# S5 over pairs of tokens, with its complex products on VectorE and other durations for the planner

## The chip, the cores and the metric

The kernel runs on one core of one Trainium2 chip. The time is the device time of one execution in microseconds (us); the median of several runs counts, and a difference of 0.2% (3.2 us) is about the least that can be told from none. A profile is taken of one further execution. Its columns of time start at the start of that execution's span.

## The reference

One layer of a hybrid streaming encoder for 256 tokens of 2048 channels, in fp32: an RMS norm, a wide input projection (w_in), three token mixers side by side (S5, HGRN2, mLSTM), a branch product for each mixer merged under sigmoid gates, an output projection, and a feed-forward part with a short causal convolution. The mixer that changes is S5, a diagonal complex state space: 32 groups of 16 channels, 64 states a group.

```
dt = exp(log_dt);  a = exp((lam_re + i lam_im) * dt)          # per group and state
c  = (a - 1) / lam;  bb = c * b                                # complex
x_t = bb @ u_t                                                 # 16 channels -> 64 states
s_t = a * s_{t-1} + x_t                                        # 256 tokens
y   = Re(c_out @ s) + d * u;  y = gelu(y);  y = y * sigmoid(y @ w_glu + b_glu)
```

## The kernel before

**Main work.** Every product with a large weight runs in three fp32r matmuls: SP loads a block of the weight (raw), ScalarE rounds it to a high half (wh, `act` at L115), VectorE subtracts to get the low half (wl, `tt` at L123), and TensorE adds high x high, high x low and low x high into a PSUM bank (mp). Blocks of 8 x 128 rows ("subs") follow one another; the halves of a block are made two blocks ahead (SPLIT), and loads run three jobs ahead (LOAD). Each engine works through its own queue in the order in which the program was written, so an early side instruction with a late input holds up what stands behind it.

**Side work.** The mixers are Python generators (`s5`, `hgrn`, `ml_...`). Between main matmuls, `pump` takes the next step of the first generator that can go on, as long as the planner's clock of VectorE or ScalarE is not more than LEAD = 2.25 us ahead of TensorE's. This clock (`Clock`, and the costs in `act`, `cost`, `scan`, `mm`, `transpose`) exists only while the program is written; it decides the order of the instructions and nothing else. `until(eng, t)` makes a generator wait till the planned clock of an engine reaches t. `drain(name)` empties a generator before a job that needs its result: the S5 results (yah, yal) are needed by the first `branch_job` of branch "a", the HGRN2 results by branch "b".

**S5.** The scan over complex states is made real by turning: with a = mag e^{i th}, the states are turned back by th t, scanned with the real mag, and turned forward. GpSimd computes the parameters (`s5_parameters`, with pw, the cosines and sines of th, 2 th, 4 th and so on), the scaled output matrix Cw, and three of four tables of cos(th t), sin(th t) for 256 tokens (`table`, one for each quarter q of the states, 4 blocks of 128); VectorE makes the first table. For each quarter, `stack` lays out u three times (high, low, high) in fp32r beside the input matrix s5b, so that TensorE gets an fp32-like product in one fp32r matmul (`emit_bu`, 4 for each half quarter). Each of eight half quarters ("units") then takes, on VectorE, four products of 128x512 from PSUM (m1, m2), two sums, four scans of 256 tokens and two products of 128x1024, and on GpSimd two sums; `c_products` multiplies with Cw (output of 32 rows for each block, four blocks side by side in TensorE), `skip` adds d u. GELU, the gate (w_glu, fp32) and the split into yah and yal end S5; the HGRN2 generator goes on after it.

**Beside S5** run the first 42 jobs: u, HGRN2's f and q, V, mLSTM's cx and v, and the first eight gates. Their results leave PSUM in late steps on VectorE (times R1) and ScalarE.

Of the kernel before, what the change touches and what calls it, by code (L numbers as in the profile page):

```python
# [17 lines left out]
LN_EXP = "natural_log_exp_and_others"  # L18

P = 128  # L20
# [28 lines left out]
class Clock:  # L49


    def __init__(self):
        self.t = {"pe": 0.0, "act": 0.0, "dve": 0.0, "pool": 0.0}

# [13 lines left out]
def hybrid_trunk(ctx: ExitStack, tc: tile.TileContext, a, dbg=None, stop=None):  # L68
# [5 lines left out]
    POWERS_AT = 25.0  # L74
# [63 lines left out]
    def scan(out, d0, d1, init, op0, op1, after=0.0):  # L138
        nc.vector.tensor_tensor_scan(out=out, data0=d0, data1=d1, initial=init, op0=op0, op1=op1)  # L139
        return ck.run("dve", after, 0.08 + 0.0021 * width(out))  # L140

    def mm(out, lhsT, rhs, start, stop, after=0.0):
        nc.tensor.matmul(out, lhsT, rhs, start=start, stop=stop)  # L143
        per = 0.000425 if lhsT.dtype == F32R else 0.0017
        return ck.run("pe", after, 0.002 + per * width(rhs))

    def transpose(out, in_, ident, after=0.0):
        nc.tensor.transpose(out, in_, ident)  # L148
        return ck.run("pe", after, 0.22)
# [51 lines left out]
    def split(job, c0, n):  # L201
        raw = job["raw"]
        wh = sb([P, RAW // 2], F32R, "wh", bufs=3)
        wl = sb([P, RAW // 2], F32R, "wl", bufs=3)
        t = act(wh[:, :n], raw[:, c0:c0 + n], AF.Copy)
        tt(wl[:, :n], raw[:, c0:c0 + n], f32(wh[:, :n]), SUB, after=t)
        return wh, wl

    gens = []

# [20 lines left out]
    def drain(name, key=None):  # L231
# [3 lines left out]

        while open_yet():
            before = dict(ck.t)
            pump(upto=name)
            if before == ck.t and open_yet():
# [3 lines left out]
                else:  # L243
                    raise RuntimeError(f"{name} waits for what never comes")

    def until(eng, t):
        while ck.t[eng] < t:
            yield "wait"
# [6 lines left out]
    LOAD, SPLIT, LEAD = 3, 2, 2.25  # L255

    def run_jobs():
# [32 lines left out]
        for i, (j, k) in enumerate(subs):  # L290
# [12 lines left out]
            wh, wl = parts[i]  # L303
            parts[i] = None
            work = job["subs"][k][2](wh, wl)
# [92 lines left out]

    def total(out, ps):
# [7 lines left out]
    def project():  # L407
# [3 lines left out]
        def evac_u(m):  # L411
            def f(ps):
# [3 lines left out]
                ready[f"u{m}"] = tt(v["u"][:, m, :], ps, R1, MULT, after=ck.t["pe"] - 2.6)  # L416
# [93 lines left out]
    def s5_parameters():  # L510
# [83 lines left out]
        ar, ai, cr, ci = t16("ar"), t16("ai"), t16("cr"), t16("ci")  # L594
        gt(ar, mag, pw[:, 0, 0, :], MULT)
        gs(ar, ar, -1.0, ADD)
        gt(ai, mag, pw[:, 1, 0, :], MULT)
        gt(cr, ar, lre, MULT)
# [8 lines left out]
        Cr0 = page(14, [P, 2, 16, 32], name="s5craw")  # L607
        nc.sync.dma_start(out=Cr0, in_=a["s5c"])
        ncr, nci = t16("ncr"), t16("nci")
        gs(ncr, cr, -1.0, MULT)  # L610
        gs(nci, ci, -1.0, MULT)
        Cr0 = page(14, [P, 2, 16, 32], name="s5craw")
        nc.sync.dma_start(out=Cr0, in_=a["s5c"])

        Cw = page(13, [P, 2, 16, 32], name="s5c")
        tq = page(11, [P, 16, 32], name="s5cq")
        for o, x0, x1 in ((0, cr, nci), (1, nci, ncr)):
            gt(Cw[:, o], Cr0[:, 0], bc(x0.unsqueeze(2), [P, 16, 32]), MULT)
            gt(tq, Cr0[:, 1], bc(x1.unsqueeze(2), [P, 16, 32]), MULT)
            gt(Cw[:, o], Cw[:, o], tq, ADD)  # L620
        v["s5"] = (mag, pw, Cw, POWERS_AT)

    def s5():
        mag, pw, Cw, tp = v["s5"]
        tabs = {}

        def table(q, tm, eng="pool"):
            tb = half(q % 2, "s5tab").rearrange("p (r b) t -> p r b t", r=2)
            e = nc.vector if eng == "dve" else nc.gpsimd
            e.memset(tb[:, 0, :, 0:1], 1.0)  # L630
            e.memset(tb[:, 1, :, 0:1], 0.0)
            for j in range(8):
                n = 1 << j
                c, s = (bc(pw[:, x, j, 4 * q:4 * q + 4].unsqueeze(2), [P, 4, n]) for x in (0, 1))
                for x, y, op in ((0, 1, SUB), (1, 0, ADD)):
                    new = tb[:, x, :, n:2 * n]
                    tt(tm[:, :, :n], tb[:, y, :, 0:n], s, MULT, eng=eng, after=tp)
                    tt(new, tb[:, x, :, 0:n], c, MULT, eng=eng)
                    t = tt(new, new, tm[:, :, :n], op, eng=eng)
                if eng == "dve":  # L640
                    yield
            tabs[q] = (tb, t)

        yield from until("dve", tp)
        yield from table(0, page(9, [P, 4, P], name="s5tm"), "dve")
        BT = page(14, [P, 1536], name="s5bt")
        braw, tm = BT[:96, :1024], BT[:, 1024:].rearrange("p (b t) -> p b t", b=4)
        for _ in table(1, tm):
            pass
        yg = v["u"]  # L650
        units = [(q, h) for q in range(4) for h in range(2)]
        bu, wg = {}, []

        stacked = {}

        def stack(q):

            nc.sync.dma_start(out=braw, in_=a["s5b"][:, q])
            us = page((3, 6)[q % 2], [96, 4, T], F32R, name="s5us")
            bs = page(12, [96, 2, 4, P], F32R, name="s5bs")  # L660
            uh, ul = scratch(dt=F32R, name="s5uh"), scratch(name="s5ul")
            t = act(uh, v["u"][:, q, :], AF.Copy)
            yield from until("dve", t)
            t = tt(ul, v["u"][:, q, :], f32(uh), SUB)
            for x in (0, 2, 1):
                for b in range(4):
                    part = ul if x == 1 else v["u"][:, q, :]
                    t = act(us[32 * x:32 * x + 32, b, :], part[32 * b:32 * b + 32, :], AF.Copy, after=t if x == 1 else 0.0)
                    yield
            bsf = bs.rearrange("p r b n -> p (r b n)")  # L670
# [3 lines left out]
            stacked[q] = (us, bs, max(t, t2))  # L674
            yield

        def emit_bu(i):
            q, h = units[i]
            if h == 0:
                yield from wait_for(f"u{q}")  # L680
                yield from stack(q)
            us, bs, t = stacked[q]
            yield from until("pe", t)
            banks = yield from side(2)
            out = [b.rearrange("p (r t) -> p r t", r=2) for b in banks]
            for b in range(2):
                for r in range(2):
                    mm(out[b][:, r, :], bs[:, r, 2 * h + b, :], us[:, 2 * h + b, :], True, True)
            bu[i] = (banks, out)

        def c_products(q, ss, tdone):
            yield from until("pe", tdone)
            bank = yield from side()
            yps = bank[:, :T]
            for r in range(2):
                for b in range(4):
                    mm(yps[32 * b:32 * b + 32, :], Cw[:, r, 4 * q + b, :], ss[b // 2][:, r, b % 2, :], r == 0, r == 1)
            v["ypre"] = (bank, yps, q, ck.t["pe"])
# [7 lines left out]
        yield from emit_bu(0)  # L706
        pend, ss = None, []
        for i, (q, h) in enumerate(units):
            tb, ttab = tabs[q]
            yield from until("dve", ttab)  # L710
            if pend is not None:
                yield from c_products(*pend)
                pend = None
            m1 = page(8 + i % 2, [P, 2, 2, T], name="s5m1")
            for b in range(2):
                cb = bc(tb[:, 0, 2 * h + b, :].unsqueeze(1), [P, 2, T])
                tt(m1[:, :, b, :], bu[i][1][b], cb, MULT, after=ck.t["pe"])
                yield
            m2 = page(10 + i % 2, [P, 2, 2, T], name="s5m2")
            for b in range(2):  # L720
                sbb = bc(tb[:, 1, 2 * h + b, :].unsqueeze(1), [P, 2, T])
                tt(m2[:, :, b, :], bu[i][1][b], sbb, MULT)
                yield
            shut(*bu.pop(i)[0])
            if i == 5:
# [3 lines left out]
            if i + 1 < len(units):  # L729
                yield from emit_bu(i + 1)  # L730
            else:
                for j, pg in enumerate((12, 10)):
# [6 lines left out]
            for r in range(2):  # L739
                for b in range(2):  # L740
                    blk = 4 * q + 2 * h + b
                    scan(m2[:, r, b, :], bc(mag[:, blk:blk + 1], [P, T]), m1[:, r, b, :], 0.0, MULT, ADD)
                    yield
            cb = bc(tb[:, 0, 2 * h:2 * h + 2, :].unsqueeze(1), [P, 2, 2, T])
            sbb = bc(tb[:, 1, 2 * h:2 * h + 2, :].unsqueeze(1), [P, 2, 2, T])
            tt(m1, m2, cb, MULT)
            yield
            t = tt(m2, m2, sbb, MULT)
            tt(m1[:, 0], m1[:, 0], m2[:, 1], SUB, eng="pool", after=t)
            t = tt(m1[:, 1], m1[:, 1], m2[:, 0], ADD, eng="pool")  # L750
            ss.append(m1)
            if h == 1:
                pend, ss = (q, ss, t), []
                if q + 2 < 4:
                    for _ in table(q + 2, tm):
                        pass
# [8 lines left out]
        for m in range(4):  # L765
# [5 lines left out]
            tp = ck.t["pe"]  # L771
            yield from until("act", tp)
            sg = scratch(name="sg")
# [3 lines left out]
            t = tt(sg, sg, yg[:, m, :], MULT)  # L777
            t = act(v["yah"][:, m, :], sg, AF.Copy, after=t)
            yield
            tt(v["yal"][:, m, :], sg, f32(v["yah"][:, m, :]), SUB, after=t)  # L780
# [542 lines left out]
    def first_norm(load_to, split_to):  # L1323
# [53 lines left out]
        ck.t = {"pe": 9.7, "act": 20.0, "dve": 21.0, "pool": 31.0}  # L1377
# [164 lines left out]
```

## Time and profile before

| | us |
|---|---|
| runs, median of 3 | 1590.81 (1589.32 to 1590.94) |
| the profiled execution | 1589.37 |
| its span | 1587.6 |
| TensorE busy | 1544.3 (97%) |
| VectorE busy | 1122.9 (71%) |
| ScalarE busy | 863.9 (54%) |
| GpSimd busy | 235.0 (15%) |

In the profile PE is TensorE, DVE is VectorE, ACT is ScalarE, POOL is GpSimd and SP the engine that issues most loads. PEclk is the clock that TensorE was granted as a share of 2.4 GHz. An fp32 matmul appears as two records, an fp32r matmul or a transpose as one. In names, s5m are S5's products and states, s5tab its tables, xp the PSUM banks of side work. An idle stretch of an engine is put down to what ended it.

### The profile page before, as it was taken

How to read it: one execution, taken by the hardware profiler on the slowest of the kernel's cores; microseconds unless marked ns; L12 is line 12 of the kernel's file. 1: busy time of each engine (PE TensorE's matmuls, PEld its weight loads, DVE VectorE, ACT ScalarE, POOL GpSimd, SP SyncE). 2: the span in 40 equal slices, each digit the busy share in tenths (PEclk: the TensorE clock that was granted, in tenths of full speed). 3: DMA queues.
4: the chain of work that ended last, by engine and by line, in shares of the span. 5: the costliest groups of instructions: out<-in, count | busy, mean ns of one | idle time of the engine just before them, and what ended most of it. 6: DMA issues, size and time to landing. Idle time of an engine off the chain costs nothing.

```text
span 1587.6 us, 25383 instructions
## 1 busy us (share of the span) xinstructions
PE 1544.3 (97%) x10094; PEld 1406.4 (89%) x10094; DVE 1122.9 (71%) x1638; ACT 863.9 (54%) x1260; POOL 235.0 (15%) x343
## 2 busy tenths in 40 slices
PE   8989889999999999999999999999999999999996
PEld 8989889899899999899888888888888888888886
DVE  7899989687653667576667777777777776454454
ACT  5555355666645557455556555555555565444442
POOL 7967862000000000000110000000000000010110
PEclk9999999999999999999999999999999999999998
DMA  7445445444455444556555555555555555555552
GB/s 266 175 166 176 138 166 186 148 150 142 155 186 212 143 143 160 179 192 241 187 187 184 187 191 191 191 191 188 187 186 186 186 187 188 176 199 177 198 183 100
DMA packets 42375, 284.71 MB, mean 179 GB/s; under 512 B 4865, under 2 KB 5249, under 8 KB 12305
## 3 DMA queue, kind: packets, MB, share of 16 engines
q1 hardware_dynamic: 40336, 276.25, 50.3%
q0 software_dynamic: 1056, 5.34, 1.0%
q8 instruction: 79, 1.29, 0.3%
q10 hardware_dynamic: 864, 1.50, 0.3%
q14 instruction: 40, 0.32, 0.1%
HBM read 280.98 MB, written 2.10 MB: 178 GB/s over the span
## 4 chain that ended last, share of the span: by engine, by line
PE 91%; DVE 5%; ACT 2%; DMA 1%; issue 1%; DVEq 0%; SPq 0%; ACTq 0%
PE mp L143 86%; PE xp L143 5%; DVE wl L123 2%; DMA raw<-w_in 1%; DVE s5m L123 1%; DVE s5m L139 1%; ACT wh L115 1%; DVE cv L135 0%; ACT L115 0%; DVE s5bs L123 0%; PE xp L148 0%; DVE x L123 0%; ACT s5bs L115 0%; ACT s5us L115 0%; DVEq L1537 0%
## 5 line engine op out<-in xcount | busy, mean ns | idle before, releaser
L123 DVE TENSOR_TENSOR wl<-raw,wh 128x1024 fp32r<-128x1024 f32 (+2 forms) x532 | 644.2, 1212 | 402.9 <-ACT wh L115 398.8
L115 ACT ACTIVATE wh<-raw 128x1024 fp32r<-128x1024 f32 (+2 forms) x532 | 549.7, 1034 | 640.8 <-PE mp L143 547.3
L143 PE MATMUL mp<-HX,wh 128*128 128x512 f32 (+1 forms) x3072 | 882.3, 354 | 1.8 <-ACT wh L115 1.2
L143 PE MATMUL mp<-HX,wl 128*128 128x256 f32 x2496 | 687.2, 283 | 15.1 <-DVE wl L123 15.1
L143 PEld LDWEIGHTS mp<-HX,wh 128*128 128x128 f32 x3072 | 535.7, 190 | 76.2 <-ACT wh L115 1.8
L143 PEld LDWEIGHTS mp<-HX,wl 128*128 128x128 f32 x2496 | 472.0, 189 | 27.9 <-DVE wl L123 17.7
L143 PE MATMUL mp<-g,wh 128*128 128x512 f32 (+1 forms) x748 | 246.3, 382 | 0.0
L143 PE MATMUL mp<-g,wl 128*128 128x256 f32 x704 | 195.4, 281 | 0.0
L143 PEld LDWEIGHTS mp<-g,wh 128*128 128x128 f32 x748 | 136.7, 188 | 28.1
L143 PE MATMUL mp<-wh,HX 128*128 128x256 f32 (+1 forms) x768 | 141.1, 284 | 0.0
L143 PEld LDWEIGHTS mp<-g,wl 128*128 128x128 f32 x704 | 132.5, 188 | 1.3
L143 PEld LDWEIGHTS mp<-wh,HX 128*128 128x128 f32 x768 | 120.3, 190 | 0.8 <-issue 0.4
L143 PE MATMUL mp<-wl,HX 128*128 128x256 f32 (+1 forms) x384 | 108.9, 284 | 4.2 <-DVE wl L123 4.2
L143 PE MATMUL mp<-m,wh 128*128 128x512 f32 x256 | 88.6, 394 | 0.0
L135 DVE SCALAR_TENSOR_TENSOR upc<-up,cols,upc 128x255 f32<-128x255 f32 (+1 forms) x176 | 84.6, 480 | 3.1
L1183 POOL COPY ACC<-sq 128x256 f32<-128x256 f32 x2 | 1.8, 908 | 518.9 <-ACT sq L115 518.9
L143 PEld LDWEIGHTS mp<-wl,HX 128*128 128x128 f32 x384 | 73.3, 191 | 4.9 <-DVE wl L123 4.8
L123 POOL TENSOR_TENSOR ACC<-ACC,sq 128x256 f32<-128x256 f32 x28 | 33.6, 1199 | 262.0 <-ACT sq L115 262.0
L143 PE MATMUL mp<-m,wl 128*128 128x256 f32 x256 | 69.3, 281 | 0.0
L115 ACT ACTIVATE upc<-up,cols 128x256 f32<-128x256 f32 x88 | 53.0, 602 | 11.2 <-DVE up L123 11.2
L143 PEld LDWEIGHTS mp<-m,wh 128*128 128x128 f32 x256 | 47.1, 188 | 9.8
L115 ACT ACT_TABLE_LOAD x41 | 52.6, 1283 | 0.9 <-DVE cv L135 0.2
(293 smaller groups left out, 1517.4 us busy)
## 6 DMA issues: line engine op xcount, KB each, us to landing
raw<-w_in SPq DMA_DIRECT2D x90, 1024.0 KB, 4.8
raw<-w_up SPq DMA_DIRECT2D x88, 1024.0 KB, 4.8
raw<-w_down SPq DMA_DIRECT2D x32, 1024.0 KB, 4.9
raw<-w_out SPq DMA_DIRECT2D x16, 1024.0 KB, 4.9
raw<-w_down SPq DMA_DIRECT2D x16, 768.0 KB, 4.2
raw<-w_bb SPq DMA_DIRECT2D x8, 768.0 KB, 4.2
raw<-w_bc SPq DMA_DIRECT2D x8, 768.0 KB, 4.3
raw<-w_ba SPq DMA_DIRECT2D x4, 1024.0 KB, 5.0
```

The source lines that it names most:

```text
L115: nc.scalar.activation(out=out, in_=in_, func=func, **kw)
L123: e.tensor_tensor(out=out, in0=in0, in1=in1, op=op)
L135: nc.vector.scalar_tensor_tensor(out=out, in0=in0, scalar=s, in1=in1, op0=op0, op1=op1)
L139: nc.vector.tensor_tensor_scan(out=out, data0=d0, data1=d1, initial=init, op0=op0, op1=op1)
L143: nc.tensor.matmul(out, lhsT, rhs, start=start, stop=stop)
L1183: nc.gpsimd.tensor_copy(out=ACC, in_=sq)
```

## The change

S5 runs over pairs of tokens. Only every second state (after an odd token) is scanned: with s_k = a^2 s_{k-1} + (a b u_even + b u_odd), 128 steps instead of 256; the input product adds a second matrix, Ba = a b (tile s5as, made by transposing on TensorE from a matrix s5bl scaled on VectorE). Outputs of odd tokens come from the states with Cw; outputs of even tokens from the state before with Ca = Cw a, and from their own input with CB = Cw B, a block-diagonal matrix made once by TensorE and masked. u is stored with even tokens first. The tables have 128 columns, two of 8 blocks, both made by VectorE, and so are all complex products; GpSimd keeps only the parameters, a few memsets and the loads of s5b and w_glu. A quarter is worked on as a whole. Output products and input products have 128 columns instead of 256.

The planner gets other durations, counts table loads of ScalarE (1.28), sets TensorE's clock to given times for the first five blocks and at least to the time when wl is ready, and adds 0.6 us (MARGIN) to every wait for TensorE outside `drain`.

```diff
-    POWERS_AT = 25.0
+    POWERS_AT, SCALED_AT = 34.0, 45.0
-        return ck.run("act", after, 0.11 + 0.00083 * width(in_) + 0.09 * len(kw))
+        load = 1.28 if table not in (None, ck.table) else 0.0
+        return ck.run("act", after, 0.18 + 0.00086 * width(in_) + 0.1 * len(kw) + load)
-        return (0.21 if n <= 64 else 0.08 + per * n) if eng == "dve" else 0.3 if n <= 64 else 0.25 + 1.9 * per * n
+        return (0.2 if n <= 64 else 0.15 + per * n) if eng == "dve" else 0.35 if n <= 64 else 0.3 + 2 * per * n
-        return ck.run("dve", after, 0.08 + 0.0021 * width(out))
+        return ck.run("dve", after, 0.13 + 0.00215 * width(out))
-        per = 0.000425 if lhsT.dtype == F32R else 0.0017
-        return ck.run("pe", after, 0.002 + per * width(rhs))
+        cost = 0.004 + 0.000445 * n if lhsT.dtype == F32R else max(0.224, 0.00168 * n)
-        while ck.t[eng] < t:
+        while ck.t[eng] < t + (margin[0] if eng == "pe" else 0.0):
+    FIRST = (9.5, 13.0, 19.1, 20.4, 23.8)
+            ck.t["pe"] = max(ck.t["pe"], FIRST[i] if i < len(FIRST) else t)
...
-        Cr0 = page(14, [P, 2, 16, 32], name="s5craw")
-        nc.sync.dma_start(out=Cr0, in_=a["s5c"])
...
+        def table(i, tm):
...
+            for j in range(7):
                 n = 1 << j
+                c, s = (bc(pw[:, x, j + 1, 8 * i:8 * i + 8].unsqueeze(1).unsqueeze(3), [P, 2, 8, n]) for x in (0, 1))
+                old, new, z = tb[:, :, :, 0:n], tb[:, :, :, n:2 * n], tm[:, :, :, :n]
+                tt(z, old, s, MULT, after=tp)
+                tt(new, old, c, MULT)
+                yield
+                tt(new[:, 0], new[:, 0], z[:, 1], SUB)
+                tt(new[:, 1], new[:, 1], z[:, 0], ADD)
+                yield
...
+        yield from times(Ba, Bl, aa)
...
+        yield from times(Cw, Cr0, cc)
...
+        yield from times(Ca, Cw, aa)
...
+        for q in range(4):
+            for r in range(2):
+                mm(ps[:, q, :], Bl[:, r, 4 * q:4 * q + 4, :].rearrange("p b n -> p (b n)"),
+                   Cw[:, r, 4 * q:4 * q + 4, :].rearrange("p b n -> p (b n)"), r == 0, r == 1)
+        tt(CBu, ps, bc(mask.unsqueeze(1), [P, 4, P]), MULT, after=ck.t["pe"])
...
-            nc.sync.dma_start(out=braw, in_=a["s5b"][:, q])
+            nc.gpsimd.dma_start(out=braw, in_=a["s5b"][:, q])
+            for r in range(2):
+                t2 = act(thrice[r], bc(Ba[:, r, 4 * q:4 * q + 4, :].unsqueeze(2), [P, 4, 3, 32]), AF.Copy)
+            yield from until("pe", t2)
+            banks = yield from side(2)
+            for r in range(2):
+                for b in range(4):
+                    transpose(banks[r][:96, b * P:(b + 1) * P], thrice[r][:, b].rearrange("p c n -> p (c n)"), ident)
...
+            for r in range(2):
+                af = as_[:, r].rearrange("p b n -> p (b n)")
+                t2 = act(af, banks[r][:96], AF.Copy)
+                yield from until("dve", t2)
+                t2 = tt(af[64:96], banks[r][64:96], f32(af[64:96]), SUB)
...
+            for r in range(2):
+                for b in range(4):
+                    mm(out[r][:, b, :], as_[:, r, b, :], us[:, b, :H], True, False)
+                    mm(out[r][:, b, :], bs[:, r, b, :], us[:, b, H:], False, True)
...
+            mm(yps[:, 0, :], CBu[:, q, :], yg[:, q, :H], True, False)
             for r in range(2):
                 for b in range(4):
+                    mm(yps[32 * b:32 * b + 32, 0, 1:], Ca[:, r, 4 * q + b, :], ss[:, r, b, :H - 1], False, r == 1)
+            for r in range(2):
+                for b in range(4):
+                    mm(yps[32 * b:32 * b + 32, 1, :], Cw[:, r, 4 * q + b, :], ss[:, r, b, :], r == 0, r == 1)
...
+            for m, x in ((m1, cs), (m2, sn)):
+                for r in range(2):
+                    tt(m[:, r], out[r], x, MULT, after=ck.t["pe"])
+                    yield
...
-            tt(m1[:, 0], m1[:, 0], m2[:, 1], SUB, eng="pool", after=t)
-            t = tt(m1[:, 1], m1[:, 1], m2[:, 0], ADD, eng="pool")
+            tt(m1[:, 0], m1[:, 0], m2[:, 1], SUB)
+            yield
+            t = tt(m1[:, 1], m1[:, 1], m2[:, 0], ADD)
...
-        ck.t = {"pe": 9.7, "act": 20.0, "dve": 21.0, "pool": 31.0}
+        ck.t = {"pe": 9.7, "act": 22.8, "dve": 25.9, "pool": 45.0}
...
-    nc = _bacc.Bacc("TRN2", target_bir_lowering=False, num_devices=1)
+    nc = _bacc.Bacc("TRN2", target_bir_lowering=False, num_devices=1, dynamic_dma_scratch_size=4096)
```

## Rows read from the trace of the kernel before

**Rows 1.** The page, part 1: busy time, share of the span, instructions

```profile
PE 1544.3 (97%) x10094; PEld 1406.4 (89%) x10094; DVE 1122.9 (71%) x1638; ACT 863.9 (54%) x1260; POOL 235.0 (15%) x343
```

**Rows 2.** Table by stretch; the last three columns are granted clock, DMA share, GB/s

```profile
60.00:112.00 52.00, 44.89 (x350) 43.38 (x349) 44.34 (x43) 31.16 (x51) 43.61 (x56) 0.97 0.45 158
112.00:156.00 44.00, 43.97 (x378) 43.08 (x377) 40.96 (x56) 24.37 (x37) 25.42 (x43) 1.00 0.56 195
156.00:184.00 28.00, 21.78 (x171) 20.29 (x169) 26.89 (x23) 10.88 (x13) 21.82 (x19) 0.94 0.34 122
212.00:244.00 32.00, 26.66 (x212) 25.15 (x212) 31.36 (x32) 13.66 (x24) 14.05 (x9) 0.95 0.46 161
284.00:316.00 32.00, 28.29 (x210) 26.72 (x209) 19.52 (x29) 17.58 (x24) 2.69 (x2) 1.00 0.33 120
544.00:556.00 12.00, 9.90 (x70) 9.50 (x69) 8.93 (x17) 6.27 (x9) 0.00 (x0) 0.86 0.30 107
556.00:1572.00 1016.00, 1016.00 (x5992) 897.86 (x5992) 688.52 (x1063) 551.98 (x820) 36.47 (x32) 1.00 0.54 184
```

**Rows 3.** TensorE's waits, 60 to 316 us: total, times, longest

```profile
PE mp L143 <- DVE wl L123: 16.5, 13, 3.1
...
PE xp L143 <- ACT u L115: 2.1, 1, 2.1
```

**Rows 4.** Timeline: start, length, engine, line, operation; VectorE and GpSimd

```profile
98.39 2.06 DVE L123 TENSOR_TENSOR wl<-raw,wh 128x1024 fp32r<-128x1024 f32 x1
...
97.47 1.90 POOL L123 TENSOR_TENSOR s5bt<-s5tab,s5pw 128x512 f32<-128x512 f32 x1
...
118.58 1.28 DVE L123 TENSOR_TENSOR s5m<-s5m,s5m 128x512 f32<-128x512 f32 x2
...
120.50 1.20 DVE L123 TENSOR_TENSOR wl<-raw,wh 128x1024 fp32r<-128x1024 f32 x1
...
121.62 1.27 DVE L139 TENSOR_TENSOR_SCAN s5m<-s_mag,s5m 128x256 f32<-128x256 f32 x2
```

**Rows 5.** Groups by form, 0 to 300 us: busy us, mean ns, idle before

```profile
L115 ACT ACTIVATE wh<-raw 128x1024 fp32r<-128x1024 f32 x82 | 86.4, 1057 | 99.3 <-PE mp L143 88.4 <-PE xp L143 5.3 <-issue 3.0
...
L123 DVE TENSOR_TENSOR s5tm<-s5tab,s5pw 128x16 f32<-128x16 f32 x2 | 0.4, 192 | 0.0
```

**Rows 6.** Chain of work that ended last, in order of time: start, length, what

```profile
31.24 2.84 PE mp L143 x24
...
77.61 0.48 PE xp L143 x4
...
131.99 1.00 PE xp L143 x16
...
321.43 2.68 PE xp L143 x24
...
329.92 2.62 PE xp L143 x24
...
522.59 0.44 PE xp L148 x4
```

**Rows 7.** Timeline of VectorE's S5 work, and the first branch product on TensorE

```profile
79.48 2.48 DVE L123 TENSOR_TENSOR s5m<-xp,s5tab 128x512 f32<-128x512 f32 x4
...
134.29 2.47 DVE L123 TENSOR_TENSOR s5m<-xp,s5tab 128x512 f32<-128x512 f32 x4
...
149.18 1.87 DVE L123 TENSOR_TENSOR s5m<-xp,s5tab 128x512 f32<-128x512 f32 x3
...
163.17 3.23 DVE L123 TENSOR_TENSOR s5m<-s5m,s5m 128x512 f32<-128x512 f32 x2
...
240.91 2.48 DVE L123 TENSOR_TENSOR s5m<-xp,s5tab 128x512 f32<-128x512 f32 x4
...
302.23 0.28 PE L143 MATMUL mp<-yah,wh 128*128 128x256 f32 x1
```

**Rows 8.** The page, part 6, DMA issues: queue, count, KB each, us to landing

```profile
wglu<-w_glu POOLq DMA_DIRECT2D x2, 512.0 KB, 5.6
```

More of the change, by code (lines that the diff above doesn't have):

```diff
@@ L621, in s5_parameters @@
-        v["s5"] = (mag, pw, Cw, POWERS_AT)
-    def s5():
[L624 to L632, printed above, removed]
-                n = 1 << j
[L634 to L642, printed above, removed]
-        yield from until("dve", tp)
[L645 to L649, printed above, removed]
@@ new lines, in s5_parameters, with times @@
+        CB = page(13, [P, 1536], name="s5c")
+        CM = page(15, [P, 1024 + P], name="s5ca")
+        BA = page(11, [P, 1536], name="s5ba")
+        mask = CM[:, 1024:]
+        nc.gpsimd.memset(mask, 0.0)
+        for b in range(4):
+            nc.gpsimd.memset(mask[32 * b:32 * b + 32, 32 * b:32 * b + 32], 1.0)
+        v["s5"] = (mag2, pw, Bl, Cr0, (a0, ai), (cr, ci), BA, CB, CM, POWERS_AT)
+    def s5():
+        mag2, pw, Bl, Cr0, aa, cc, BA, CB, CM, tp = v["s5"]
+        Ba, Cw, Ca = (x[:, :1024].rearrange("p (r g n) -> p r g n", r=2, g=16) for x in (BA, CB, CM))
+        spare, mask, CBu = BA[:, 1024:], CM[:, 1024:], CB[:, 1024:].rearrange("p (q n) -> p q n", q=4)
+        H = T // 2
+        def table(i, tm):
+            tb = half(i, "s5tab").rearrange("p a t -> p (a t)").rearrange("p (r b t) -> p r b t", r=2, b=8)
+            nc.vector.memset(tb[:, 0, :, 0:1], 1.0)
+            nc.vector.memset(tb[:, 1, :, 0:1], 0.0)
+            for j in range(7):
+                n = 1 << j
+                c, s = (bc(pw[:, x, j + 1, 8 * i:8 * i + 8].unsqueeze(1).unsqueeze(3), [P, 2, 8, n]) for x in (0, 1))
[6 more added lines that the diff above has]
+                yield
+            return tb
+        yield from until("dve", tp)
+        tm = page(9, [P, 2, 8, H // 2], name="s5tm")
+        tabs = []
+        for i in range(2):
+            tabs.append((yield from table(i, tm)))
+        z = page(8, [P, 2, 16, 32], name="s5z")
+        def times(out, x, s):
+            sr, si = (bc(y.unsqueeze(1).unsqueeze(3), [P, 2, 16, 32]) for y in s)
+            tt(z, x, si, MULT, after=SCALED_AT)
+            yield
+            tt(out, x, sr, MULT)
+            yield
+        yield from times(Ba, Bl, aa)
+        tt(Ba[:, 0], Ba[:, 0], z[:, 1], SUB)
+        tt(Ba[:, 1], Ba[:, 1], z[:, 0], ADD)
+        yield
+        yield from times(Cw, Cr0, cc)
+        tt(Cw[:, 0], Cw[:, 0], z[:, 1], SUB)
+        stt(Cw[:, 1], Cw[:, 1], -1.0, z[:, 0], MULT, SUB)
+        yield
+        yield from times(Ca, Cw, aa)
+        tt(Ca[:, 0], Ca[:, 0], z[:, 1], ADD)
+        t = tt(Ca[:, 1], Ca[:, 1], z[:, 0], SUB)
+        yield
+        yield from until("pe", t)
+        bank = yield from side()
+        ps = bank.rearrange("p (q n) -> p q n", q=4)
+        for q in range(4):
[3 more added lines that the diff above has]
+        tt(CBu, ps, bc(mask.unsqueeze(1), [P, 4, P]), MULT, after=ck.t["pe"])
+        shut(bank)
+        yield
@@ L673, in stack, with emit_bu @@
             t2 = tt(bsf[64:96], braw[64:96], f32(bsf[64:96]), SUB)
-            stacked[q] = (us, bs, max(t, t2))
+            stacked[q] = (us, as_, bs, max(t, t2))
             yield
[L677 to L682, printed above, removed]
+        def emit_bu(q):
+            yield from wait_for(f"u{q}")
+            yield from stack(q)
+            us, as_, bs, t = stacked[q]
             yield from until("pe", t)
             banks = yield from side(2)
[L685 to L689, printed above, removed]
+            out = [b.rearrange("p (b t) -> p b t", b=4) for b in banks]
+            for r in range(2):
+                for b in range(4):
+                    mm(out[r][:, b, :], as_[:, r, b, :], us[:, b, :H], True, False)
+                    mm(out[r][:, b, :], bs[:, r, b, :], us[:, b, H:], False, True)
+            return banks, out
         def c_products(q, ss, tdone):
@@ L704, in skip @@
             shut(bank)
[L706 to L710, printed above, removed]
+        bu = yield from emit_bu(0)
+        pend = None
+        for q in range(4):
+            tb = tabs[q // 2]
+            cs, sn = (tb[:, x, 4 * (q % 2):4 * (q % 2) + 4, :] for x in (0, 1))
             if pend is not None:
                 yield from c_products(*pend)
[L713 to L725, printed above, removed]
+            banks, out = bu
+            m1 = page(8 + q % 2, [P, 2, 4, H], name="s5m1")
+            m2 = page(10, [P, 2, 4, H], name="s5m2")
+            for m, x in ((m1, cs), (m2, sn)):
+                for r in range(2):
+                    tt(m[:, r], out[r], x, MULT, after=ck.t["pe"])
+                    yield
+            shut(*banks)
+            if q == 2:
                 ready["us2"] = ck.t["dve"]
@@ L1499, in _layouts @@
             c[64 * e:64 * e + 64, r, g // 2, 16 * e:16 * e + 16] = cw[g].T
-    o["s5b"], o["s5c"] = b.reshape(96, 4, 1024), c
+            bl[64 * e:64 * e + 64, r, g // 2, 16 * e:16 * e + 16] = bw[g]
+    o["s5b"], o["s5bl"], o["s5c"] = b.reshape(96, 4, 1024), bl, c
     parts = {
```

108 lines of the change are left out of this document (58 added, 50 removed).

## The prediction

> **What bounds the kernel now.** I read four views, in this order. The page's busy line gives TensorE 97% of the span [rows 1], so only its gaps and its slow stretches can be won back, and whatever the change adds to TensorE is paid in full. The table by stretch says where the gaps are [rows 2]: in the feed-forward part, from 556 to 1572, there is no idle time at the full 2.4 GHz, and that thousand microseconds cannot move. The loss sits in the S5 part: 7.1 us idle from 60 to 112, 6.2 from 156 to 184, 5.3 from 212 to 244, together 18.7. In the same three stretches the granted clock averages 0.97, 0.94 and 0.95, TensorE being put to 1.2 GHz after each longer gap: 0.03 x 52 + 0.06 x 28 + 0.05 x 32 = 4.8 us of work done later. From 284 to 316 another 3.7 us are idle, and round 550 there are 2.1 idle and 0.14 x 12 = 1.7 at the low clock. The waits say for whom: 16.5 us of the gaps wait for VectorE's low half wl of a weight block, and one of 2.1 for S5's GELU on ScalarE [rows 3]. The timeline says why wl is late. The same wl took 2.06 us beside GpSimd's 1.90 us table product and 1.20 where GpSimd was silent [rows 4]. From 112 to 156, mostly quiet, TensorE lost 0.03 us [rows 2]. So it is not the amount of VectorE work that stops TensorE but its stretching by GpSimd, which the planner's costs do not know.
>
> **The change, part by part.** The sum is made against the profiled execution: span 1587.6, 1.8 around it, 1589.4 in all. The median shown is 1590.8; it lies 1.4 above.
>
> *GpSimd falls silent in S5.* Tables and the last complex products go to VectorE, and GpSimd keeps the parameters, which end near 55 us. VectorE then works at quiet durations: about 0.20 us for 16 columns [rows 5], 0.64 for 512, 1.20 for 1024, and 0.40 for a scan of 128 columns (half of the 0.64 that 256 take, and 0.08 for its fixed part) [rows 4].
>
> *VectorE's work changes in kind, hardly in amount.* New: two tables, each of seven steps of four products (three steps all short at 0.8 each, then 1.0, 1.4, 2.2, 3.7) = 10.7, so 21.4; scaling by three times two products of 1024 and two of 512, 3 x 3.7 = 11.2; per quarter four products from PSUM, two sums, eight scans, two wide products, two sums, 8 x 0.64 + 8 x 0.40 + 2 x 1.20 = 10.7, so 43; splits 4 x 2.9, skip and GLU 5, some 17; 93 in all. Before, at quiet durations: one table on VectorE near 13, 32 + 16 operations of 512 at 0.64 (31), 32 scans (20), 16 wide ones (19), and some 12 of the rest: 95. Equal within the guess. What goes is the stretching, and with it the three lossy stretches: 18.7 + 4.8 = 23.5 us. I leave 2.5 of that standing (bounds 0, as from 112 to 156, and 8, a third of today's), because side work still shares VectorE's queue with wl, two blocks ahead. Gain 21.0.
>
> *TensorE pays.* A quarter's eight input products took two times 0.48 us for four, 0.12 each [rows 6]; they become sixteen of 128 columns. No row has this kind at 128 columns. From below it is half, 0.06; from above a plain fp32 product of 128 columns, twelve in 2.68 us as 24 records, 0.22. Nearest are records of 64 columns with the same 128-wide weights: 24 in 2.62, 0.109 each [rows 6], so halving columns stops paying at the weights, and I take 0.109: 64 x 0.109 = 7.0 against 32 x 0.12 = 3.8, +3.1 (0 to +10). The output products took 1.00 us for 16 records, four column groups side by side, 63 ns a record [rows 6]. They become 32 records of half the columns and one 128-wide product of 0.22. If columns set the 63 ns, a quarter costs 1.0 + 0.2; if the instruction does, 2.0 + 0.2. I take the second, since 256 fp32 columns in two passes over four groups would fill only some 53 of the 63 ns: 8.9 against 4.0, +4.9 (+0.9 to +4.9).
>
> The Trainium skill ("TensorE: Matmul & The Clock Gate", section "Wait — 56ns, not 53.3ns?") says that with hardware decode off the sequencer spends about 62 ns on each matmul, and that this binds once the array's work is shorter. By it the output products stay at 2.0 a quarter; by a reading of the row as pure column time they would be 1.0, and the total 4 us lower. The trace's 63 ns agrees with the rule, but no run here shows which decode is on.
>
> Then 32 transposes at 0.11 (four in 0.44 [rows 6]) = 3.5, and eight fp32 products of 128 columns for CB at 0.22 = 1.7. TensorE in all +13.2 (bounds +6 and +20).
>
> *ScalarE* gets, per quarter, two copies of 384 and two of 512 columns, some 2.2 us at the rate of the 1024-wide copy's 1057 ns [rows 5]. It is idle near half the time here, and this counts only through S5's end, next.
>
> *The moment S5 is due.* The first branch product (yah) starts at 302.2 [rows 7]; everything that S5 still owes by then is issued with no main work between. With the gains and TensorE's additions it moves to 302.2 - 21.0 - 2.1 + 13.2 = 292. When is S5 through? A block of main work is 24 matmuls in 2.84 us [rows 6], of which wl and its share of evacuations hold VectorE for about 1.4, so side work gets 0.51 of it; the half quarter from 134.3 to 149.2 [rows 7] got ten operations of 0.64, two of 1.20 and one of 0.4, 9.2 us, into 14.9, 0.62. At 0.53: tables and scaling from 34 on, 33/0.53 = 62, to 96; CB to 100. A stack took from 149.2 + 3.1 to 163.2 [rows 7], 11 us; with the transposes and copies about 16: 116. A quarter is then 10.7/0.53 + 16 + 2 of waiting for its output products = 38 (today 54, three from 79.5 to 240.9 [rows 7]); three of them to 230, the last without a stack to 252, and GELU, GLU and splits 15 to 27 more: 267 to 279, 13 to 25 ahead. At 0.51 with stacks of 19 it is 285 to 297, on time or 5 late. The planner's own costs put it nearer the second, since they overcharge the output products (17 x 0.224) and add a margin of 0.6 to every TensorE step. I take 4.0 us of waiting here in place of today's 2.1: -2.0.
>
> *The reckoning elsewhere.* New durations, table loads and the margin change only the order of issue. From 316 on side work is HGRN2 and mLSTM. Table loads now counted should soften the stall round 550 (2.1 + 1.7): +1.5 (bounds 0 and 3.8). Of the 1.6 us left from 284 to 316 I give back 0.8. The start, full on TensorE until 60, I leave.
>
> *Loads.* The per-quarter matrix s5b goes from SP's queue to GpSimd's, where 512 KB land in 5.6 us [rows 8]; the stack's copies before its use cover it, and SP's weight loads no longer queue behind its buffer. The constants are two loads of 512 KB as before (s5c was loaded twice), early, while TensorE has no gap. If the smaller descriptor space made GpSimd's loads twice as long, each still has more than 10 us of cover.
>
> Sum: 21.0 - 13.2 - 2.0 + 0.8 + 1.5 = 8.1 us. 1589.4 - 8.1 = 1581.3; I say 1581.5.
>
> **The rivals.** *Late at the branch.* S5 starts its quarters some 35 us later than today (116 against 79), behind two full tables and the scaling. For it: the second reckoning above. Against it: quarters of 38 instead of 54. It decides once S5 owes over 12 us at the first branch product (4 charged, 8.1 gained): the tail is a chain through ScalarE, TensorE and VectorE, nothing hides it, and TensorE falls to 1.2 GHz behind it. With 20 owed: 16 + 1.7 - 8.1, about 1599. Owing 8 to 15 ends within 0.2%.
>
> *Narrow products at the full fp32 rate.* If those of 128 columns take 0.22, TensorE gets 64 x 0.11 = 7 more: 1588.5, no change. For it: nothing here shows the fast rate below 256 columns. Against it: nothing either, save that weights alone explain 0.109.
>
> *The stretching was not it.* If wl was late because the planner ran TensorE 6% too fast, the new durations cure the same gaps, and the time is the forecast's. If neither cures them, half of the 23.5 stays and TensorE still pays: 1589.4 - 11.8 + 13.2 - 0.3 = 1590.5.
>
> *Everything lands well.* Output products scale with columns, S5 is early, no stall is left: 8.1 + 4 + 4 + 2.5, about 1570.
>
> **How the numbers follow.** Forecast 0.50 (its own range 1575 to 1587); all lands well 0.12; late by a lot 0.16, by a little 0.11; narrow products at full rate 0.06; the gaps not cured 0.05. This kernel's measurement tells 0.2%, 3.2 us, from no change, so 1587.6 to 1594.0 is the same: the little lateness, the narrow products, half of the uncured gaps, 0.19; slower 0.18 with the other half; faster 0.63. The range leaves out below 1567 (0.07) and above 1597 (0.12).
>
> **What would show it.** In the changed kernel's trace: no 2 us wl after 60 us; idle time and low clock of TensorE from 60 to the first branch product under 5 us together; sixteen input products in about 1.75 us and the output products in 2.2; quarters 38 us apart; the first yah product near 292. It is wrong if TensorE idles over 10 us just ahead of that product, if wl still waits, or if the side products take over 20 us more than today.

## The result and the profile after

The kernel after takes 1569.88 us (median of 4 runs, 1568.86 to 1573.23), the kernel before 1590.07 beside it (1589.18 to 1590.94): ratio 0.9882, 95% interval 0.9867 to 0.9897, 20.2 us less. Forecast were 1581.5, 9.3 less. The direction, the place and the mechanism were right; the size was half of what came, and the time is that of the rival "everything lands well", which had a chance of 0.12. Its sum fits by luck: it adds 4, 4 and 2.5 us to the forecast's gain, which came as 4.0, 2.5 and 2.5, and the other terms of the account below happen to make up the rest. The profiled execution took 1570.68 (span 1568.9), 18.7 less than that of before; the account below is made against these two.

The page's busy line after, for [rows 1]:

```profile
PE 1543.4 (98%) x10246; PEld 1410.0 (90%) x10246; DVE 1084.9 (69%) x1645; ACT 878.3 (56%) x1281; POOL 98.5 (6%) x179
```

TensorE has 152 records more and is busy 0.9 us less: what it gained was time in which it had stood still or run slowly. GpSimd went from 235 to 98.5. The table by stretch, for [rows 2] (busy time and instructions of PE, PEld, DVE, ACT, POOL, then granted clock, DMA share, GB/s):

```profile
60.00:112.00 52.00, 52.00 (x439) 52.00 (x439) 42.84 (x67) 29.30 (x43) 0.00 (x1) 1.00 0.50 170
112.00:156.00 44.00, 44.00 (x375) 44.00 (x375) 35.48 (x47) 28.40 (x44) 1.02 (x2) 1.00 0.58 195
156.00:184.00 28.00, 28.00 (x261) 27.68 (x260) 23.26 (x39) 17.73 (x30) 0.51 (x1) 1.00 0.50 177
212.00:244.00 32.00, 32.00 (x294) 31.68 (x294) 27.50 (x39) 20.41 (x28) 1.08 (x2) 1.00 0.61 203
244.00:284.00 40.00, 38.61 (x316) 36.87 (x314) 26.28 (x41) 21.82 (x29) 3.25 (x3) 1.00 0.44 161
284.00:316.00 32.00, 31.05 (x263) 30.71 (x263) 26.93 (x33) 19.29 (x20) 0.81 (x1) 1.00 0.40 134
316.00:544.00 228.00, 224.52 (x1720) 215.60 (x1720) 143.90 (x196) 132.37 (x188) 3.44 (x7) 0.99 0.48 168
```

The three lossy stretches have no idle time left and the full clock. TensorE's waits from 60 to 316 us (total, times, longest), for [rows 3]:

```profile
PE xp L148 <- ACT u L117: 0.9, 1, 0.9
PE mp L148 <- DVE merged L128: 0.9, 1, 0.9
PE mp L148 <- ACT yah L117: 0.5, 1, 0.5
```

No wait for wl stands there, where 16.5 us did. VectorE's wl by form, 60 us to the first branch product (busy, mean ns, idle before), for [rows 4]:

```profile
L128 DVE TENSOR_TENSOR wl<-raw,wh 128x1024 fp32r<-128x1024 f32 x65 | 79.5, 1223 | 37.9 <-ACT wh L117 37.5
```

Pieces of the chain that ended last (start, length, what), for [rows 6], and the first branch product, for [rows 7]:

```profile
121.15 1.74 PE xp L148 x16
...
127.20 0.87 PE xp L157 x8
...
156.94 1.23 PE xp L148 x34
...
195.51 1.23 PE xp L148 x34
...
242.46 1.23 PE xp L148 x34
...
266.82 1.23 PE xp L148 x34
```

```profile
281.70 0.47 PE L148 MATMUL mp<-yah,wh 128*128 128x256 f32 x1
```

Sixteen input products take 1.74, a quarter's output products with CB 1.23, and the first branch product starts at 281.7 instead of 302.2, so the whole gain is there by then. From it to the end of the span the kernel after takes 1287.2 us against 1285.4, 1.8 more.

### The profile page after: what moved, and what is told of

Read it like the earlier page. It is cut to its first block, busy times and chain, and to the rows that moved or that the text cites. A ratio compares the mean times of both kernels' runs of the same rounds, so it can differ in the third digit from the quotient of the medians.

```text
span 1568.9 us, 25533 instructions
## 1 busy us (share of the span) xinstructions
PE 1543.4 (98%) x10246; PEld 1410.0 (90%) x10246; DVE 1084.9 (69%) x1645; ACT 878.3 (56%) x1281; POOL 98.5 (6%) x179
## 4 chain that ended last, share of the span: by engine, by line
PE 97%; DMA 1%; ACT 1%; DVE 1%; issue 0%; DVEq 0%; SPq 0%; ACTq 0%
PE mp L148 91%; PE xp L148 5%; DMA raw<-w_in 1%; PE xp L157 0%; ACT wh L117 0%; ACT L117 0%; DVE x L128 0%; DVE wl L128 0%; DVEq L1604 0%; ACT rows L117 0%; ACT u L117 0%; DVE HX L140 0%; ACT o L117 0%; ACT ybh L117 0%; ACT rw L117 0%
## 5 line engine op out<-in xcount | busy, mean ns | idle before, releaser
L128 DVE TENSOR_TENSOR wl<-raw,wh 128x1024 fp32r<-128x1024 f32 (+2 forms) x532 | 634.2, 1192 | 427.4 <-ACT wh L117 424.3
L117 ACT ACTIVATE upc<-up,cols 128x256 f32<-128x256 f32 x88 | 53.0, 603 | 11.6 <-DVE up L128 11.4
L148 PEld LDWEIGHTS mp<-m,wl 128*128 128x128 f32 x256 | 48.2, 188 | 1.3
```

Of the source, the lines that this page charges most:

```text
L128: e.tensor_tensor(out=out, in0=in0, in1=in1, op=op)
```

## The experiments

**Planner or S5?** The first undoes the planner's part of the change in the kernel after, the second makes that part alone in the kernel before. Of the first:

```diff
-        return ck.run("act", after, 0.18 + 0.00086 * width(in_) + 0.1 * len(kw) + load)
+        return ck.run("act", after, 0.11 + 0.00083 * width(in_) + 0.09 * len(kw))
...
-        while ck.t[eng] < t + (margin[0] if eng == "pe" else 0.0):
+        while ck.t[eng] < t:
...
-        ck.t = {"pe": 9.7, "act": 22.8, "dve": 25.9, "pool": 45.0}
+        ck.t = {"pe": 9.7, "act": 20.0, "dve": 21.0, "pool": 31.0}
```

> The changed S5 with the planner of before (its durations, no margin, no table loads, its starting clocks). If GpSimd's stretching of VectorE was what stopped TensorE, the gain stands without the new durations: TensorE waits under 3 us for wl from 60 us to the first branch product, and the time is 1569 to 1576. If the old durations were the cause (TensorE planned 6% too fast), more than 8 us of waits for wl come back and the time is 1580 to 1588.

> S5 of before with the planner of after alone. If GpSimd's stretching was the cause: wl of 2 us beside GpSimd's products stay, more than 12 us of waits for wl stay between 60 and 316, and the time is 1586 to 1594. If the durations were the cause: the waits for wl fall under 5 us and the time is 1573 to 1582, or lower, since TensorE gets none of the change's additions.

Measured: 1572.56 (ratio to before 0.9909, 0.9891 to 0.9928) and 1589.79 (1.0012, 1.0002 to 1.0023). S5's new form alone brings 16 to 17 us; the durations alone bring nothing, and 2.7 on top of the new S5, which the spread of the runs hardly tells from none. The planner as the cause is out. TensorE's waits from 60 to 316 in the second kernel show why nothing came: some waits for wl went (10.9 are left, a little under the 12 expected), others took their place.

```profile
PE mp L148 <- DVE wl L128: 10.9, 9, 2.6
PE xp L148 <- POOL s5m L128: 4.6, 2, 4.0
PE xp L148 <- DVE s5m L128: 3.2, 2, 2.7
PE xp L148 <- ACT u L117: 1.7, 1, 1.7
```

**GpSimd put back, without its use.** 48 products that nothing reads, in the kernel after; then memsets in their place.

```diff
...
+        def load_pool(q):
+            nc.gpsimd.tensor_copy(out=gpl[0:1, 0:1], in_=f32(stacked[q][0][0:1, 0, 0:1]))
+            for _ in range(16):
+                nc.gpsimd.tensor_tensor(out=gpl, in0=gpl, in1=gpo, op=MULT)
...
         bu = yield from emit_bu(0)
+        load_pool(0)
...
                 bu = yield from emit_bu(q + 1)
+                if q < 2:
+                    load_pool(q + 1)
```

> The kernel after with 48 GpSimd products of 128x512 added in S5, 16 beside each of the first three quarters, which nothing reads and nothing waits for. If GpSimd stretches VectorE: each takes 1.3 to 1.9 us, wl beside them takes near 2 us instead of 1.2, waits for wl come back (before lost 18.7 us in stretches with some 79 us of GpSimd work; here there are 65 to 90, with less VectorE work owed beside them, so 6 to 18 us), and the time is 1576 to 1590. If it does not stretch, or VectorE's slack covers it: under 2 us of waits and the time of the kernel after, 1568 to 1573.

> As the run with 48 GpSimd products, but with 180 memsets of 128x512 in their place, 60 beside each of the first three quarters: GpSimd as busy, but reading nothing. If any GpSimd access to SBUF stretches VectorE, wl beside them takes 1.7 to 2.0 us and the time is 1576 to 1586, as with the products (1584). If it is the reading of operands, wl stays at 1.2 and the time at 1568 to 1573.

The products (66.9 us in 48) bring 1584.05 (0.9979, 0.9968 to 0.9990), 14.2 more than after, and 6.4 us of waits for wl with the low clock behind them (0.94 from 156 to 212); the load of s5b, held up behind the products, cost 0.8 of waits. VectorE by form in that kernel, 106 to 155 us, nearly all of it beside GpSimd:

```profile
L128 DVE TENSOR_TENSOR wl<-raw,wh 128x1024 fp32r<-128x1024 f32 x12 | 19.4, 1624 | 7.1 <-ACT wh L117 7.0
L136 DVE TENSOR_SCALAR f<-f,lb,lb 128x256 f32<-128x256 f32 x5 | 4.7, 974 | 0.0
L128 DVE TENSOR_TENSOR s5bs<-s5br,s5bs 32x1024 fp32r<-32x1024 f32 x2 | 3.9, 1948 | 0.1
L144 DVE TENSOR_TENSOR_SCAN s5m<-s_mag,s5m 128x128 f32<-128x128 f32 x3 | 3.4, 1178 | 0.0
L128 DVE TENSOR_TENSOR s5m<-s5m,s5m 128x512 f32<-128x512 f32 x2 | 3.0, 1524 | 0.0
L128 DVE TENSOR_TENSOR s5as<-xp,s5as 32x512 fp32r<-32x512 f32 x4 | 2.6, 684 | 0.1
L128 DVE TENSOR_TENSOR s5m<-xp,s5tab 128x512 f32<-128x512 f32 x4 | 2.5, 684 | 0.0
```

Operations with both inputs in SBUF are stretched: s5m<-s5m,s5m takes 1524 ns (684 in the kernel after), a scan of 128 columns 1178 (405 there), s5bs 1948 (1218); those that read one input from PSUM (xp) stay at 684. The Trainium skill ("SBUF — State Buffer", section "Who interferes with whom") says that a VectorE instruction with two SBUF inputs contends with a GpSimd instruction that reads SBUF, and not with one that only writes it. For operations with two tensors in SBUF both halves of it agree with these runs: beside memsets from 106 to 212 us wl is not stretched. One operation falls under neither half: f, which reads one tensor from SBUF and two columns of scalars (lb), takes 974 ns beside the products and 647 beside the memsets, where the kernel after has 411. Why it is stretched by both stays open; it is 5 operations in these stretches, where wl, on which TensorE waits, is 12 and 26.

```profile
L128 DVE TENSOR_TENSOR wl<-raw,wh 128x1024 fp32r<-128x1024 f32 x26 | 31.7, 1221 | 18.4 <-ACT wh L117 18.0
...
L136 DVE TENSOR_SCALAR f<-f,lb,lb 128x256 f32<-128x256 f32 x5 | 3.1, 647 | 0.0
```

Still the memsets came to 1581.49 (0.9951, 0.9935 to 0.9968), inside the range expected of the first theory, but for a reason that neither had: the load of s5b stands in GpSimd's queue behind 60 memsets, was issued at 140.4 (at 121.0 in the kernel after), and TensorE waited once for what is made of it:

```profile
PE xp L148 <- DVE s5bs L128: 6.8, 1, 6.8
```

So the 11.6 us of that run are a late load and the low clock behind the gap (0.71 from 142 to 148, 0.58 from 148 to 156), not a stretched VectorE.

**The loss of before, measured.** Three of the four tables and the sums that GpSimd does for S5 left out of the kernel before, first with its own planner, then with the new one. The scaling of Cw, six GpSimd products of 512 columns, stays in.

```diff
...
+            if eng == "pool":
+                for j in range(8):
+                    for _ in range(6):
+                        t = ck.run("pool", tp, cost("pool", 4 << j, 0.00104))
+                tabs[q] = (tabs[0][0], t)
+                return
...
-            tt(m1[:, 0], m1[:, 0], m2[:, 1], SUB, eng="pool", after=t)
-            t = tt(m1[:, 1], m1[:, 1], m2[:, 0], ADD, eng="pool")
+            t = ck.run("pool", t, cost("pool", 2 * T, 0.00104))
+            t = ck.run("pool", 0.0, cost("pool", 2 * T, 0.00104))
```

> The kernel before, with GpSimd's part of S5 left out: three of the four tables are not computed (the first stands in for them) and the last two sums of each half quarter are skipped; the planner counts them as if they were there, so the order of all else is that of before. What goes is GpSimd beside VectorE, and nothing is put in its place. If the stretching is the whole loss of the three stretches and the busy rows size it right (18.7 idle and 4.8 at the low clock), the time is 23.5 lower, near 1566.5. If the same rows read by counts of records are right (27.0 lost), it is near 1563. If GpSimd's stretching is not the cause, the time stays above 1580.

> The kernel before with GpSimd's part of S5 left out, as in the run that came to 1568.1, and with the planner of after. That run still lost 4.1 us idle and 1.6 at the low clock from 60 to 156 behind a stack of ScalarE copies in front of wh. If this remainder is the old durations' doing, it goes, and the time is 1561 to 1565. If the new planner gives nothing to S5 of before, as with GpSimd at work (1589.8 against 1588.9), the time is 1567 to 1571.

Measured: 1568.10 (0.9863, 0.9846 to 0.9881) and 1572.63 (0.9879 to 0.9926). The first is the cleanest proof of the mechanism: VectorE and TensorE do the same work in the same order, GpSimd is nearly silent once Cw is scaled (66 us), and 21.2 us are gone. Nor were they waits for GpSimd's results: by the profile's waits neither TensorE nor VectorE of the kernel before waited for GpSimd from 60 to 316 us. The time does not settle at either figure expected, because a loss stays from 60 to 156 us:

```profile
60.00:112.00 52.00, 48.80 (x394) 48.59 (x395) 41.13 (x53) 34.62 (x56) 5.94 (x4) 0.97 0.51 181
112.00:156.00 44.00, 43.13 (x371) 42.23 (x370) 38.47 (x50) 25.92 (x38) 0.00 (x0) 1.00 0.54 185
156.00:184.00 28.00, 28.00 (x243) 27.28 (x242) 26.66 (x38) 10.08 (x10) 0.00 (x0) 1.00 0.52 178
```

That is 3.2 + 0.9 idle and 0.03 x 52 = 1.6 at the low clock, 5.7; with the 21.2 it makes 26.9. What the second run was expected to test, that this remainder comes from a stack of copies on ScalarE, is a misreading of the first. All but 1.1 of the 5.7 follow from one wait at the start, which the kernel before has too. TensorE's waits from 60 to 70 us, VectorE's wl from 55 to 68, and GpSimd beside it:

```profile
PE mp L143 <- DVE wl L123: 3.0, 1, 3.0
...
L123 DVE TENSOR_TENSOR wl<-raw,wh 128x1024 fp32r<-128x1024 f32 x3 | 6.0, 2031 | 0.0
...
61.77 2.02 POOL L123 TENSOR_TENSOR s5cq<-s5craw,s_ncr 128x512 f32<-128x512 f32 x1
```

These wl take 2.03 us beside the scaling of Cw, which was left in, and the low clock lies behind that gap (0.65 from 64 to 68). So 3.0 + 1.6 of the remainder is GpSimd's as well. In the kernel after VectorE scales Cw and the gap is gone; with the new planner but GpSimd's scaling (the second run) it is there again, 3.1. That run missed both figures expected and is 4.5 slower than the first, for which the record gives no cause. ScalarE's stack (eleven copies, 98.0 to 102.7 us) explains 0.3 us.

**Output products.** Each cut into two of 64 columns.

```diff
...
+            for c0, c1 in ((0, 64), (64, H)):
+                for r in range(2):
+                    for b in range(4):
+                        nc.tensor.matmul(yps[32 * b:32 * b + 32, 1, c0:c1], Cw[:, r, 4 * q + b, :], ss[:, r, b, c0:c1],
+                                         start=r == 0, stop=r == 1)
...
```

> The kernel after with each output product of 128 columns cut into two of 64, in the same order for the planner: 66 records a quarter instead of 34. If the columns set the time of these products, a quarter's stay at 1.2 to 1.4 us and the time changes by under 1 us. If 32 ns is the least that such a record takes, they need 2.1 us, 0.9 a quarter more, 3.6 in all: 1572 to 1575. If an instruction takes about 62 ns whatever its columns, 4.1 us a quarter, 11.5 in all: 1580 to 1583.

Measured: 1569.98 (0.9894, 0.9872 to 0.9916), no difference to the kernel after. The chain in that kernel, one quarter:

```profile
156.58 0.22 PE xp L148 x2
156.80 0.58 PE xp L770 x32
157.38 0.45 PE xp L775 x32
```

64 records in 1.03 us, 16 ns each, where 32 of 128 columns take 1.23 - 0.22 = 1.01, 32 ns each, and 256 columns took 63 [rows 6]. Columns set the time of these products, down to 64.

**Input products.** Each cut into two of 64 columns; then, as a counterpart, each issued twice at 128.

```diff
...
+                    for c in (0, 64):
+                        nc.tensor.matmul(out[r][:, b, c:c + 64], as_[:, r, b, :], us[:, b, c:c + 64], start=True, stop=False)
+                        nc.tensor.matmul(out[r][:, b, c:c + 64], bs[:, r, b, :], us[:, b, H + c:H + c + 64], start=False, stop=True)
...
```

> The kernel after with each input product of 128 columns cut into two of 64: 32 records a quarter instead of 16, the same columns in all. If the weights set the 0.109 us of such a record, a quarter takes 3.5 us instead of 1.74, 7.0 more in all: 1575 to 1578. If columns set it, as they do for the output products (34 records or 66 in the same 1.2 us), the time of the kernel after: 1569 to 1571.

> The kernel after with each pair of input products issued twice, at the full 128 columns: 32 records a quarter, as many and as long a block as in the run with 64 columns, but twice its columns. At 0.109 us a record 7.0 us more of TensorE in all. If the granted clock fell in the run with 64 columns because such a block holds few columns for its length, it stays at 1.00 here and the time is 1576 to 1578. If the length of a block of side products is what made it fall, it falls here too, and the time is 1581 to 1585.

With 64 columns 1583.84 (0.9961, 0.9946 to 0.9975), 14.0 more than after; twice at 128 columns 1578.93 (0.9948, 0.9928 to 0.9968), 9.1 more, 0.9 above the range expected, its profiled span 7.2 longer. In both profiles a record takes 0.11 us, so columns do not set it. That the 128-wide weights do, as the prediction had it, fits, and no run tests it apart; 64 records more cost 7.0. The other 7 us of the first are clock. TensorE there, table by stretch and then the chain:

```profile
122.00:126.00 4.00, 4.00 (x39) 1.00 0.56 166
126.00:130.00 4.00, 4.00 (x23) 0.57 0.53 207
...
240.00:244.00 4.00, 4.00 (x26) 0.68 0.81 262
```

```profile
147.02 0.11 PE xp L758
147.14 0.20 PE xp L759
```

TensorE shows no idle time there, yet it fell to 1.2 GHz behind the block that ran from 122.5 to 126.1, again inside the next one (0.11 a record turns to 0.20) and behind the last; behind the third (186.0 to 189.4) it did not. 0.12 x 44 + 0.05 x 32 = 6.9 us from 112 to 156 and 212 to 244. In the profile with as many records of 128 columns the clock stayed at 1.00 from 60 to 316. That is one execution of each: over all runs the mean granted clock is 0.989 to 0.993 with 64 columns, 0.991 to 0.997 twice at 128 and 0.994 to 0.997 after, and the two longest runs of the second (1581.7 and 1582.0 us) are those at 0.991. So whether its clock never falls is not shown.

**The planner's two sizes, and a stall that was left.** LEAD 1.75; MARGIN 0; and mLSTM's gate rows:

```diff
-        ta = act(fg, fg, AF.Abs, after=t)
-        ta = act(fg, fg, AF.Exp, scale=-1.0, after=ta)
-        ta = act(fg, fg, AF.Ln, bias=1.0, after=ta)
+        ta = act(F, fg, AF.Abs)
+        yield
+        nc.scalar.preload_act_table_set(LN_EXP)
+        ta = act(F, F, AF.Exp, scale=-1.0, after=ta)
+        ta = act(F, F, AF.Ln, bias=1.0, after=ta)
+        yield
...
```

> The kernel after with LEAD 1.75 instead of 2.25: side work runs less far ahead of TensorE. If the stalls that are left from 316 to 544 (3.5 us: side work and table loads on ScalarE in front of wh) come from too much side work in front, they shrink and the time falls by 1 to 3: 1567 to 1569. If S5 is late by it, TensorE waits ahead of the first branch product and the time is 1572 to 1585.

> The kernel after with MARGIN 0 in place of 0.6. If the margin is what the new planner gives (the run with the old planner lost 2.7), waits for TensorE's side products come in front of VectorE's wl again: 1 to 3 us of stalls from 60 to 280, 1571 to 1573. If the durations alone do, 1569 to 1570.

> The kernel after with mLSTM's gate rows in other steps: the absolute value goes to a free row, so that ScalarE does not wait for VectorE in front of wh; one table load serves the exponential and the logarithm; and two yields let wh of the next block come between. The stall at 527 us (1.9 and 0.5 idle, and 0.83 and 0.95 of the clock for 16 us behind it, 1.8) should go: 2 to 4 us less, 1566 to 1568. If the next block's wh is held up by something else there, the time stays at 1569 to 1570.

Measured: 1569.69 (0.9859 to 0.9889), 1570.23 (0.9869 to 0.9906) and 1565.97 (0.9860, 0.9838 to 0.9881). Neither size matters here. The last is below both kernels: its runs, 1565.2 to 1566.8, lie under all of the kernel after. Its waits of TensorE from 316 to 560:

```profile
PE mp L148 <- ACT gate L117: 1.1, 1, 1.1
```

## Why it came out so, step by step

The step that failed is the size of two terms of the sum, not the mechanism. The output products were charged 2.0 us a quarter and took 1.0, 4.0 us in all. And what GpSimd's silence gives back was put at 21.0 us (23.5 less 2.5 left standing) and was 27.0. The two make 10.0 of the 10.6 us missed; the rest nearly cancels.

The account, against the two profiled executions (8.1 us forecast, 18.7 measured):

| step of the sum | forecast | measured | difference |
|---|---|---|---|
| loss of the three stretches before | 23.5 | 27.0 | +3.5 |
| of it left standing | 2.5 | 0 | +2.5 |
| output products and CB's part | +4.9 | +0.9 | +4.0 |
| input products, transposes, CB | +8.3 | +8.4 | 0 |
| lost from 244 to 316 (S5's end) | 4.8 | 2.3 | +2.5 |
| the start | 0 | 1.7 gained | +1.7 |
| the stall round 550 | 1.5 gained | 0 | -1.5 |
| new stalls at 366 and 559 us | 0 | 1.9 | -1.9 |

The differences add up to 10.8, where 18.7 - 8.1 = 10.6.

*GpSimd falls silent: right.* No 2 us wl is left, idle time from 60 to the first branch product is 0.9 us at the full clock (under 5 forecast), and the cause is shown from both sides: GpSimd's work taken out of before, and put into after. *Its size: too small.* The prediction summed idle time and low clock. Counting records says more, and needs no ends of matmuls. TensorE's main records of before by stretch:

```profile
60.00:112.00 52.00, 44.26 (x342) 0.97 0.45 158
...
156.00:184.00 28.00, 20.29 (x151) 0.94 0.34 122
...
212.00:244.00 32.00, 24.87 (x188) 0.95 0.46 161
```

342 records at 2.84/24 = 0.118 and 8 input products at 0.12 fill 41.4 of 52 us: 10.6 lost, not 8.7. In the same way 8.6 and 7.8 instead of 7.9 and 6.9, 27.0 in all, which the run without GpSimd's tables and sums bears out: 21.2 gone and 5.7 left. Matmul ends are modelled, so a row of busy time hides some of what a gap costs.

*What stays of it: the 2.5 left standing were not there.* The bound 0, read from 112 to 156 of before, was the right one. But that stretch was not "mostly quiet": GpSimd was busy for 25.4 of its 44 us [rows 2], and from 184 to 212 for 25.9 of 28, and TensorE lost next to nothing in either. Before from 184 to 212, its wl there, and its wl from 60 to 112:

```profile
184.00:212.00 28.00, 28.00 (x237) 28.00 (x234) 23.80 (x32) 15.31 (x25) 25.88 (x42) 1.00 0.53 172
...
L123 DVE TENSOR_TENSOR wl<-raw,wh 128x1024 fp32r<-128x1024 f32 x5 | 6.1, 1225 | 0.0
...
L123 DVE TENSOR_TENSOR wl<-raw,wh 128x1024 fp32r<-128x1024 f32 x16 | 25.3, 1584 | 7.5 <-ACT wh L115 7.5
```

From 184 to 211 GpSimd ran table products of 4 to 256 columns, and wl took 1.23; in the lossy stretches it ran most of those of 512, and wl took 1.44 to 1.58. So by these rows the price hangs on which products GpSimd runs, not on how long it is busy; no run varies their width alone.

*Output products: the step that failed by argument.* The prediction took the instruction to set the 63 ns, because columns would fill only some 53 of it, and charged 2.0 a quarter. They take 1.0: 32 ns a record of 128 columns, half of 63. The rule weighed there, from the Trainium skill ("TensorE: Matmul & The Clock Gate", section "Wait — 56ns, not 53.3ns?"), of some 62 ns on each matmul with hardware decode off, does not bind in this kernel: 16 ns a record were measured. Which decode is on, no run shows. That 63 and 62 are alike was chance.

*Input products, transposes, CB: right* (1.74, 0.87 for eight, 1.79). With them the rival of narrow products at the full fp32 rate fell; "the stretching was not it" fell with the two planner runs.

*The moment S5 is due.* The first branch product was forecast near 292 and starts at 281.7. Quarters were forecast 38 apart; the output products stand 38.6, 47.0 and 24.4 apart, the last at 266.8. GELU and GLU follow; TensorE waits 0.9 and 0.5 in place of the 4.0 charged, since the GLU's products (7.2 us) fill the rest of the tail, and no low clock follows. "Late at the branch" did not come, though S5 ended with nothing to spare.

*Round 550: wrong.* The stall did not soften; it moved with all else to 527 us (1.9 and 0.5 idle), and it is there with either planner. Its cause is the wait of ScalarE for VectorE, with two table loads behind it, in front of wh; the experiment on the gate rows removed it; which of its three edits did it, no run tells. TensorE's waits after, from 316 to 560, with the two new stalls of the account (gate and issue):

```profile
PE mp L148 <- ACT wh L117: 1.9, 1, 1.9
PE mp L148 <- ACT gate L117: 1.1, 1, 1.1
PE xp L148 <- issue: 0.8, 1, 0.8
PE mp L148 <- DVE wl L128: 0.5, 1, 0.5
```

In front of the gate ScalarE loads a table (1.28 us at 365.0). Why the new order puts it there stays open, and so does the other stall.

*The start* is chance: with the early code of after the profiled executions of it and its variants show 0.86, 0.93 or 1.00 for the first 24 us and 93 to 109 records. After had 14 more than before, 14 x 0.118 = 1.7.

## What to carry to other kernels

Work given to GpSimd is not free because GpSimd is idle: beside its products of 512 columns, which read SBUF, VectorE's operations with two inputs in SBUF took 1.3 to 2.9 times as long, and if these feed TensorE the price is paid there, with the low clock on top. Its busy time alone does not tell: in the stretches of before with mostly narrower products, next to nothing was lost. Size such a loss by counting the records of a stretch against the same records in a full one, not by idle time alone. And when a per-record time is to be scaled to a new shape, measure two shapes before choosing what bounds it.

## What the hardware showed unexpectedly

- The granted clock can fall to 1.2 GHz with TensorE at work all the time: behind 32 records of 64 columns at 0.11 us each it was 0.57 for 4 us (it fell in or behind three of four such blocks), behind 32 of 128 columns at the same 0.11 it stayed at 1.00 in the one execution profiled.
- VectorE's operations with one input from PSUM took 684 ns beside GpSimd's products as without them; a scan with both inputs in SBUF took 1178 instead of 405. Beside memsets these did not change, but an operation with one tensor in SBUF and two columns of scalars took 647 instead of 411.
- fp32 records with 32-row outputs, four column groups side by side, took 63, 32 and 16 ns at 256, 128 and 64 columns: no least time of an instruction shows down to 16 ns.
